# Moving the second half's x preparation into the u and g product, with GpSimd in program order during the first V product and staged scaling of B's weights

## The chip, the cores and the metric

The kernel runs on one core of one Trainium2 chip. The metric is the device time of one execution in microseconds, as the median of several runs. All times below are of that one core.

## The reference

A decoder trunk on x of 2048 tokens by 1024 features, in float32. One gated-MLP layer (A) is followed by one sliding-window attention layer (B). Cut to what matters here:

```python
h = rms_norm(x, a_norm_g)
u, v, g = split(h @ w_in, 3)            # w_in: 1024 x 6144, each part 2048 wide
v = layer_norm(v, ln_g, ln_b)           # over 2048 features
sv = einsum('gts,bcsgd->bctgd', tril(ws), v) + bs   # mixes the tokens of a chunk of 128, 16 groups
x = x + (u * sv * silu(g)) @ w_out
kv = rms_norm(x, kv_norm_g) @ w_kv + b_kv           # layer B from here
z  = rms_norm(x, b_norm_g) @ b_w_in                 # q and gate
... rotary, banded attention with sinks, gate, output product
out = rms_norm(x, final_norm_g)
```

The norm gains kv_norm_g and b_norm_g are multiplied into the weights w_kv and b_w_in ahead of layer B ("B's weights scaled").

## The kernel before

Every large product is made in three matmuls with operands split into a high part (rounded to the matmul's own type) and a low part (the rest): high times high, high times low, low times high. `split` makes them: a copy on ACT (L118) and a subtraction on DVE (L119). PE, DVE, ACT and POOL are TensorE, VectorE, ScalarE and GpSimd; SP is the queue that carries all loads, in order.

Layer A goes over the tokens in two halves of 1024. For each half come the V product, the u/g product (8 pairs of feature blocks; gate and mixing of the pair before are woven in) and the out product (4 pairs). The first V product (`vphase_first`, 768 matmuls of 128x512) works plainly on x split as it comes; the later products use Winograd's form of Strassen's 2x2 scheme: 7 products for 8, on sums and differences of quarters of x and of the weights. Those sums of quarters have to be prepared, and most of it is done beside the first V product:

- `sum_job(i)`, four of them: loads four quarters of wv into the tile pair qa, makes four sums or differences on GpSimd (`quarter_sums`) and stores them (su) for the V product of the second half.
- `x_steps(0, k)`: x of the first half, rebuilt from its high and low part on GpSimd (L448) and multiplied by the norm factor on DVE (L449), then 7 stores of plain quarters and their combinations (`combos`, GpSimd; X and X_s are the stores).
- `x_steps(1, k)`: the same for the second half, but loaded from memory into tile xq and normalised on DVE (L445), with the factor loaded from rx.
- `stat_steps(b)`: loads x of the second half, squares it on ACT, adds the squares on DVE (L248), and ends in `rnorm`, a chain over PE, DVE, GpSimd and ACT that gives the norm factor (L255 to L291).
- `load_consts(q)`: masks the mixing weights, forms a constant, stores 32 small pieces (wsc).

Beside the second V product (`vphase(1)`, 672 matmuls) 36 jobs `prescale(i)` scale B's weights: a multiplication on GpSimd (L496), the high part on ACT (L499), the low part on GpSimd (L502), two stores (L504).

Two things set the order. The program counts half steps: `half()` is called after each 12 matmuls and runs what `after(n, ...)` has put n half steps ahead. A scheduler then turns the program's order into one queue for each engine, by the readiness that it expects. Tiles named s come from a pool of 18 that rotates; raw weights have 12 buffers, split weights 4, and `weights()` keeps three splits ahead. The first V product is half steps 0 to 64, a u/g pair 14 half steps.

```python
        for i in range(4):
            after(6 + 6 * i, lambda i=i: sum_job(i))
```

Of the kernel before, what the change touches and what calls it, by code (L numbers as in the profile page):

```python
# [12 lines left out]
F32 = mybir.dt.float32  # L13
F32R = mybir.dt.float32r
I32 = mybir.dt.int32
AF = mybir.ActivationFunctionType
ALU = mybir.AluOpType

P = 128
# [3 lines left out]
TB = 512  # L23
# [3 lines left out]
NJ = AW // P  # L27
# [35 lines left out]
def trunk(ctx: ExitStack, tc: tile.TileContext, xT, wv, wug, wao, wkv, wqg, wbo, wsT, bs, gains, lngb,  # L63
# [12 lines left out]
    pD = [[dram.tile([P, TB], F32, name=f"p{b}_{k}", tag=f"p{b}_{k}") for k in range(KD)] for b in range(NB)]  # L76
    rxD = [dram.tile([P, TB], F32, name=f"rx{b}", tag=f"rx{b}") for b in range(NB)]
    vD = [[dram.tile([P, 2 * TT, 512], F32, name=f"v{i}_{c}", tag=f"v{i}_{c}") for c in range(4)] for i in range(2)]
    wscD = [dram.tile([P, 256], F32, name=f"wsc{j}", tag=f"wsc{j}") for j in range(NJ)]
    sumD = [[dram.tile([P, 2, 512], F32, name=f"su{i}_{n}", tag=f"su{i}_{n}") for n in range(4)] for i in range(4)]  # L80
    setD = {(s, i): {n: dram.tile([P, 4, TB], F32, name=f"{s}{i}_{n}", tag=f"{s}{i}_{n}") for n in STEPS}
            for s in ("X", "Y0_", "Y1_") for i in range(2)}
# [5 lines left out]
    def load(dst, src):  # L88
        nc.sync.dma_start(dst, src)

    def slot(dt=F32):
        return gen[0].tile([P, TB], dt, name="s", tag="s")
# [24 lines left out]
    def split(hi, lo, src, lo_eng=None):  # L117
        A.copy(hi, src)  # L118
        (lo_eng or V).tensor_tensor(lo, src, hi.bitcast(F32), ALU.subtract)  # L119
# [22 lines left out]
    def after(n, fn):  # L142
        at(now[0] + n, fn)
# [18 lines left out]
    for b in range(NB):  # L162
        for p in PIECES:
            kind, i, j = p[0], int(p[1]), int(p[2])
# [78 lines left out]
    def sumsq_step(acc, src, eng=G):  # L243
        sq = slot()
        A.activation(sq, src, AF.Square)
        if acc is None:
            return sq
        eng.tensor_tensor(acc, acc, sq, ALU.add)  # L248
        return acc
# [83 lines left out]
    with ExitStack() as actx:  # L333
# [51 lines left out]
        def load_consts(q):  # L385

            w, c = slot(), slot()
            w3 = w.rearrange("p (j t) -> p j t", j=4)
            load(w3, wsT[:, 4 * q:4 * q + 4, :])
            load(c, bs[q * 512:(q + 1) * 512].partition_broadcast(P))  # L390

            def first():
                G.affine_select(out=w3, in_=w3, pattern=[[0, 4], [1, P]], base=0, channel_multiplier=-1,
                                compare_op=ALU.is_ge, fill=0.0)

            def second():
                ps = bank()
                PE.matmul(ps, ones, w, start=True, stop=True)
                for i in range(4):
                    ts, j = slice(i * P, (i + 1) * P), 4 * q + i  # L400
                    V.scalar_tensor_tensor(c[:, ts], ps[:, ts], ln_b[:, j:j + 1], c[:, ts], ALU.mult, ALU.add)
                    G.dma_start(wscD[j][:, :P], w[:, ts])
                    G.dma_start(wscD[j][:, P:], c[:, ts])

            after(2, first)
            after(5, second)
# [17 lines left out]
        def x_steps(sb, k, tag):  # L424

            qs, its = [], []

            def begin():
                t = xcg.tile([P, 2048], F32, name="xq", tag=tag)
                qs.extend(t[:, i * TB:(i + 1) * TB] for i in range(4))  # L430
                if sb:
                    for i, z in enumerate(qs):
                        load(z, xT[2 + i // 2, k + 4 * (i % 2)])
                    rs.extend(slot() for _ in range(2))
                    for h in range(2):
                        load(rs[h], rxD[2 + h])
                else:
                    rs.extend(r0[h] for h in range(2))

            rs = []  # L440

            def norm(i):
                h, n = i // 2, k + 4 * (i % 2)
                if sb:
                    V.scalar_tensor_tensor(qs[i], qs[i], a_g[:, n:n + 1], rs[h], ALU.mult, ALU.mult)  # L445
                else:
                    hi, lo = fx[h, n]
                    G.tensor_tensor(qs[i], hi.bitcast(F32), lo.bitcast(F32), ALU.add)  # L448
                    V.tensor_tensor(qs[i], qs[i], rs[h], ALU.mult)  # L449

            def norms(h):
                norm(2 * h)
                norm(2 * h + 1)

            def step():
                if not its:
                    its.append(combos(qs[0], qs[2], qs[1], qs[3], ("X", sb), k))
                next(its[0])

            return [begin, lambda: None, lambda: norms(0), lambda: norms(1), step, step, step]  # L460

        def sum_job(i):

# [6 lines left out]
                sumD[i][n], t.rearrange("p (u c) -> p u c", u=2))))  # L470

        def quarter_sums(a11, a12, a21, a22, put):
            G.tensor_tensor(a22, a21, a22, ALU.add)
            put(0, a22)
            G.tensor_tensor(a21, a11, a21, ALU.subtract)
            put(2, a21)
            G.tensor_tensor(a11, a22, a11, ALU.subtract)
            put(1, a11)
            G.tensor_tensor(a12, a12, a11, ALU.subtract)
            put(3, a12)  # L480


# [4 lines left out]
        def prescale(i):  # L487
            src, dst, g, nk = pre_jobs[i // 2]
            nk //= 2
            z = i % 2  # L490
            w = slot()
            load(w, src[:, z * 512:(z + 1) * 512])

            def second():
                w3 = w.rearrange("p (k n) -> p k n", k=nk)
                G.tensor_tensor(w3, w3, g[:, z * nk:(z + 1) * nk, None].broadcast_to([P, nk, 512 // nk]), ALU.mult)  # L496
                for i, t in enumerate((slot(F32R), slot(F32R))):
                    if i == 0:
                        A.copy(t, w)  # L499
                        hi = t  # L500
                    else:
                        G.tensor_tensor(t, w, hi.bitcast(F32), ALU.subtract)  # L502
                for i, t in enumerate((hi, t)):
                    G.dma_start(dst[:, i * 1024 + z * 512:i * 1024 + (z + 1) * 512], t.bitcast(F32))  # L504

            after(2, second)


        def chain_of(width, product, keep, done, on_step):
# [101 lines left out]
        def load_v(sb, j):  # L611
            v = vtile().rearrange("p (c d) -> p c d", c=2 * TT)
            load(v, vD[sb][j // 4][:, :, (j % 4) * P:(j % 4 + 1) * P])
            wc = ac.tile([P, 256], F32, name="wc", bufs=3)
            load(wc, wscD[j])
            return v, wc

        def mix(j, ln, v, wc, us, sgs):
# [123 lines left out]
            fx[h, k] = hi, lo  # L742

        box = [None, None]

        def first_stat(h, k, t, wait):
            box[h] = sumsq_step(box[h], t, V)
            if k == KD - 1:
                rnorm(box[h], lambda r: r0.update({h: r}), wait, 4, lambda z: r4.update({h: z}))

# [12 lines left out]
            after(3 + k // 2, lambda k=k: first_split(1, k, ys[k]))  # L763
            after(6 + k // 2, lambda k=k: first_stat(1, k, ys[k], 2))
        for i in range(4):
            after(6 + 6 * i, lambda i=i: sum_job(i))
        for k in range(4):
            for i, f in enumerate(x_steps(0, k, ("12h", "12l")[k % 2])):
                after(18 + 6 * k + i, f)
            for i, f in enumerate(x_steps(1, k, ("s2h", "s2l")[k % 2])):  # L770
                after(38 + 6 * k + i, f)
        for b in range(2, 4):
            for i, f in enumerate(stat_steps(b)):
                after(10 + 8 * (b - 2) + i, f)
        for q in range(4):
            after(14 + 4 * q, lambda q=q: load_consts(q))
        for i, n in ((50, "11"), (53, "12"), (58, "s1"), (60, "s3"), (62, "s2")):
# [3 lines left out]
        for sb in range(2):  # L781
            if sb:
                for i in range(36):
                    after(3 + 3 * i // 2, lambda i=i: prescale(i))
                ln = vphase(sb)
            else:
                ln = vphase_first()
                load_set(("X", 0), "s4")
                load_set(("X", 0), "22")
            pend = None  # L790
            res = {}

            def ahead(kh, m, sb=sb, res=res):
                res[11] = res_loads(sb, kh, m, 11)

            for kh in range(2):
                for jj in range(4):
                    last = kh == 1 and jj == 3
                    pend = ug_pair(sb, kh, jj, ln, pend, ("Y0_", sb) if last else None, (lambda: ahead(0, 0)) if last else None)
            acc = [None, None]  # L800
            for kh in range(2):
                for m in range(2):
                    nxt = None
                    if m == 1:
                        nxt = ("Y1_", sb) if kh == 0 else ("X", 1) if sb == 0 else None
                    if sb and kh and m:
                        hn0 = ([], [])
                        for k, f in enumerate(hn_steps(0, *hn0)):
                            after(6 + k, f)
                    nx = 2 * kh + m + 1  # L810
                    out_pair(sb, kh, m, acc, nxt, pend, ln, res, (lambda: ahead(nx // 2, nx % 2)) if nx < 4 else None)
                    pend = None
            for h in range(2):
                rnorm(acc[h], lambda r, b=2 * sb + h: G.dma_start(rD[b], r))
# [419 lines left out]
```

## Time and profile before

| | us |
|---|---|
| median of 3 runs | 2284.58 |
| lowest and highest | 2279.96, 2290.11 |
| the profiled execution | 2290.78 |
| its span, from first to last instruction | 2288.9 |

| engine | busy us | share of the span |
|---|---|---|
| PE (matmul) | 2152.2 | 94% |
| DVE | 1678.9 | 73% |
| ACT | 1086.0 | 47% |
| POOL | 1137.0 | 50% |

The mean granted clock of TensorE is 0.976 of full speed, and 441.95 MB go through DMA at a mean of 193 GB/s. In the profile a group names the code line, the engine, the operation, the tiles (written to, then read from) and how often; behind the bar stand the busy time in us and the mean in ns, and last the idle time of the engine just before the group with what ended it. A row of waits names engine, tile and line that waited, what it waited for, and the total, the number and the longest. A row of transfers ends with its size in KB and the median time in us from issue to landing. Matmuls overlap, so their distance is read from their starts.

### The profile page before, as it was taken

The page shows a single profiled execution, that of the slowest core. Times are in us where ns is not written, and L with a number is a line of the kernel's source. Part 1 is how long each engine was busy: PE and PEld are TensorE (multiplying, and loading weights), DVE is VectorE, ACT ScalarE, POOL GpSimd, SP SyncE. Part 2 cuts the span into 40 slices and gives each one's busy share as a digit, 9 for nine tenths or more (in the row PEclk, how much of TensorE's full clock was granted, in tenths as well). Part 3 has the DMA queues.
Part 4 walks back from the last instruction along what each step waited for, and adds up shares of the span by engine and source line. Part 5 has one row for each costly group of instructions (what it writes and reads, how often), then busy time and mean ns, then how long its engine had stood idle before and what let it go on. Part 6 is the DMA issues. An engine that isn't in the chain of part 4 may idle for free.

```text
span 2288.9 us, 33545 instructions
## 1 busy us (share of the span) xinstructions
PE 2152.2 (94%) x11196; PEld 1816.8 (79%) x11196; DVE 1678.9 (73%) x2641; ACT 1086.0 (47%) x2431; POOL 1137.0 (50%) x1238
## 2 busy tenths in 40 slices
PE   6878899999999998999999999989999999999997
PEld 4656678888878776778888778889889889989986
DVE  8787866576888856666667788667957876895785
ACT  5322454454624533345445534436725744672673
POOL 5786535454455477955445454515513532551461
PEclk8988999999999999999999999999999999999999
DMA  7997834344777778934444677643355255336322
GB/s 275 339 334 267 310 108 157 110 153 143 239 272 252 275 244 292 315 113 152 128 136 154 213 263 250 233 158 111 116 193 181 88 195 188 111 120 219 132 93 92
DMA packets 209324, 441.95 MB, mean 193 GB/s; under 512 B 23040, under 2 KB 62208, under 8 KB 199936
## 3 DMA queue, kind: packets, MB, share of 16 engines
q1 hardware_dynamic: 163488, 255.76, 34.5%
q0 software_dynamic: 41056, 175.67, 21.1%
q10 hardware_dynamic: 4608, 8.39, 1.0%
q8 instruction: 89, 1.46, 0.3%
q14 instruction: 83, 0.68, 0.1%
HBM read 322.81 MB, written 116.92 MB: 192 GB/s over the span
## 4 chain that ended last, share of the span: by engine, by line
PE 62%; DVE 12%; DMA 11%; POOL 6%; issue 6%; ACT 3%; SPq 1%; DVEq 0%; POOLq 0%; ACTq 0%
PE ps L130 12%; PE ps L128 12%; PE ps L129 12%; PE ps L122 6%; PE ps L124 6%; PE ps L123 6%; PE ps L625 2%; DMA s<-in_xT 2%; DVE wa L119 2%; PE ps L997 2%; DMA s<-in_wqg 1%; DVE xl L119 1%; DMA s<-X_s 1%; PE ps L975 1%; POOL s L502 1%
## 5 line engine op out<-in xcount | busy, mean ns | idle before, releaser
L119 DVE TENSOR_TENSOR wa<-w_raw,wa 128x512 fp32r<-128x512 f32 x456 | 481.7, 1068 | 223.5 <-ACT wa L118 218.2
L130 PE MATMUL ps<-xh,wa 128*128 128x512 f32 x1344 | 530.3, 395 | 15.1 <-DVE wa L119 15.1
L128 PE MATMUL ps<-xh,wa 128*128 128x512 f32 x1344 | 531.7, 396 | 6.0 <-ACT s L539 4.2
L129 PE MATMUL ps<-xl,wa 128*128 128x512 f32 x1344 | 528.9, 394 | 0.0
L118 ACT CAST wa<-w_raw 128x512 fp32r<-128x512 f32 x456 | 279.4, 619 | 395.3 <-PE ps L130 296.5
L130 PEld LDWEIGHTS ps<-xh,wa 128*128 128x128 f32 x1344 | 253.7, 189 | 76.7 <-DVE wa L119 20.4
L128 PEld LDWEIGHTS ps<-xh,wa 128*128 128x128 f32 x1344 | 253.9, 189 | 62.0 <-ACT s L539 4.6
L129 PEld LDWEIGHTS ps<-xl,wa 128*128 128x128 f32 x1344 | 253.8, 189 | 55.8
L983 POOL TENSOR_SCALAR_AFFINE_SELECT s<-s 128x512 fp32r<-128x512 f32 x256 | 185.3, 752 | 101.6 <-ACT s L977 69.3
L122 PE MATMUL ps<-w,hn 128*128 128x256 f32 x640 | 184.3, 288 | 0.0
L123 PE MATMUL ps<-w,hn 128*128 128x256 f32 x640 | 182.4, 285 | 0.0
L124 PE MATMUL ps<-w,hn 128*128 128x256 f32 x640 | 182.3, 285 | 0.0
L223 POOL TENSOR_TENSOR w_raw<-w_raw 128x512 f32<-128x512 f32 x48 | 73.6, 1534 | 201.4 <-DMA w_raw<-in_wug 134.0
L123 PE MATMUL ps<-wa,xh 128*128 128x512 f32 x256 | 109.9, 429 | 43.4 <-DVE wa L119 43.4
L119 DVE TENSOR_TENSOR xl<-s,xh 128x512 fp32r<-128x512 f32 x168 | 138.8, 866 | 11.0 <-ACT xh L118 10.8
L190 POOL DMA_DIRECT2D w<-wb x72 | 40.7, 566 | 205.6 <-PE ps L124 181.5
L225 POOL TENSOR_TENSOR w_raw<-w_raw 128x512 f32<-128x512 f32 x48 | 71.0, 1482 | 124.0 <-DVE wa L119 123.9
L621 ACT ACTIVATE vp<-vp,nb,rs 128x128 f32<-128x128 f32 x256 | 106.3, 484 | 49.2 <-DMA vp<-v 35.1
L969 POOL TENSOR_TENSOR s<-s,rd 128x512 f32<-128x512 f32 x64 | 69.6, 1090 | 117.0 <-DVE rd L967 47.7
L123 PEld LDWEIGHTS ps<-w,hn 128*128 128x128 f32 x640 | 124.2, 194 | 0.5
L122 PEld LDWEIGHTS ps<-w,hn 128*128 128x128 f32 x640 | 124.0, 194 | 0.5
L124 PEld LDWEIGHTS ps<-w,hn 128*128 128x128 f32 x640 | 124.0, 194 | 0.0
(195 smaller groups left out, 5057.2 us busy)
## 6 DMA issues: line engine op xcount, KB each, us to landing
w<-wb POOLq DMA_DIRECT2D x72, 1024.0 KB, 5.4
w_raw<-in_wug SPq DMA_DIRECT2D x160, 256.0 KB, 3.1
w_raw<-in_wv SPq DMA_DIRECT2D x88, 256.0 KB, 5.8
w_raw<-in_wao SPq DMA_DIRECT2D x80, 256.0 KB, 4.2
wb<-s POOLq DMA_DIRECT2D x72, 256.0 KB, 4.8
s<-in_xT SPq DMA_DIRECT2D x64, 256.0 KB, 5.6
vp<-v SPq DMA_DIRECT2D x32, 512.0 KB, 4.4
Y_s<-s POOLq DMA_DIRECT2D x64, 256.0 KB, 3.8
```

Source lines behind the costliest of these rows:

```text
L118: A.copy(hi, src)
L119: (lo_eng or V).tensor_tensor(lo, src, hi.bitcast(F32), ALU.subtract)
L122: PE.matmul(ps, ah, bh, start=first, stop=False)
L123: PE.matmul(ps, ah, bl, start=False, stop=False)
L124: PE.matmul(ps, al, bh, start=False, stop=last)
L128: PE.matmul(ps, ah, bh, start=first, stop=False, skip_group_check=True)
L129: PE.matmul(ps, ah, bl, start=False, stop=False, skip_group_check=True)
L130: PE.matmul(ps, al, bh, start=False, stop=True, skip_group_check=True)
L223: G.tensor_tensor(u["22"], u["21"], u["22"], ALU.add)
L225: G.tensor_tensor(u["11"], u["22"], u["11"], ALU.subtract)
L621: A.activation(v[:, c, :], v[:, c, :], AF.Identity, bias=nb[:, c:c + 1], scale=rs[:, c:c + 1])
L983: G.affine_select(out=y.rearrange("p (h q) -> p h q", h=4), in_=x.rearrange("p (h q) -> p h q", h=4), pattern=[[0, 4], [sign, P]], base=ba ...
```

## The change

Four edits. (1) `x_steps(1, k)` and `stat_steps(2)`, `stat_steps(3)` are put into the first half's u/g product: the statistics into pairs 0 to 2, the preparation of x, one k for each pair, into pairs 3 to 6. Their tiles are now taken from the rotating pool s. (2) A new helper `in_turn` chains GpSimd's tensor operations in the order of the program: the sums of wv (now in two pieces of 512 columns for one of 1024), the rebuilding of x, and, for the second block of the first half, the square sums, which move from DVE to GpSimd (L770 in the changed kernel). `sum_job(i)` is put 14 + 9i half steps ahead for 6 + 6i, `x_steps(0, k)` 17 + 8k for 18 + 6k, and it has one empty step more between the tile and the normalisation. (3) `load_consts` stores 8 pieces of 256 KB for 32 of 64 KB. (4) `prescale` is taken apart: the multiplication two half steps after the load, the split a half step later, with the low part on DVE, the stores yet one later.

```diff
-    wscD = [dram.tile([P, 256], F32, name=f"wsc{j}", tag=f"wsc{j}") for j in range(NJ)]
+    wscD = [dram.tile([P, 4, 2, P], F32, name=f"wsc{q}", tag=f"wsc{q}") for q in range(4)]
...
-                    G.dma_start(wscD[j][:, :P], w[:, ts])
-                    G.dma_start(wscD[j][:, P:], c[:, ts])
+                for i, z in enumerate((w, c)):
+                    G.dma_start(wscD[q][:, :, i, :], z.rearrange("p (j t) -> p j t", j=4))
...
+                if sb == 0:
+                    t = xcg.tile([P, 2048], F32, name="xq", tag=tag)
+                    qs.extend(t[:, i * TB:(i + 1) * TB] for i in range(4))
+                else:
+                    qs.extend(slot() for _ in range(4))
...
-                    G.tensor_tensor(qs[i], hi.bitcast(F32), lo.bitcast(F32), ALU.add)
+                    in_turn(lambda: G.tensor_tensor(qs[i], hi.bitcast(F32), lo.bitcast(F32), ALU.add))
...
-            return [begin, lambda: None, lambda: norms(0), lambda: norms(1), step, step, step]
+            return [begin, lambda: None, lambda: None, lambda: norms(0), lambda: norms(1), step, step, step]
...
         def quarter_sums(a11, a12, a21, a22, put):
-            G.tensor_tensor(a22, a21, a22, ALU.add)
+            def tt(out, a, b, op):
+                for z in range(2):
+                    zs = slice(z * 512, (z + 1) * 512)
+                    in_turn(lambda: G.tensor_tensor(out[:, zs], a[:, zs], b[:, zs], op))
+
+            tt(a22, a21, a22, ALU.add)
...
-            def second():
-                w3 = w.rearrange("p (k n) -> p k n", k=nk)
-                G.tensor_tensor(w3, w3, g[:, z * nk:(z + 1) * nk, None].broadcast_to([P, nk, 512 // nk]), ALU.mult)
-                for i, t in enumerate((slot(F32R), slot(F32R))):
-                    if i == 0:
-                        A.copy(t, w)
-                        hi = t
-                    else:
-                        G.tensor_tensor(t, w, hi.bitcast(F32), ALU.subtract)
-                for i, t in enumerate((hi, t)):
-                    G.dma_start(dst[:, i * 1024 + z * 512:i * 1024 + (z + 1) * 512], t.bitcast(F32))
-            after(2, second)
+            w3 = w.rearrange("p (k n) -> p k n", k=nk)
+            gb = g[:, z * nk:(z + 1) * nk, None].broadcast_to([P, nk, 512 // nk])
+            after(2, lambda: G.tensor_tensor(w3, w3, gb, ALU.mult))
+            def third():
+                hi, lo = slot(F32R), slot(F32R)
+                split(hi, lo, w)
+                def fourth():
+                    for i, t in enumerate((hi, lo)):
+                        G.dma_start(dst[:, i * 1024 + z * 512:i * 1024 + (z + 1) * 512], t.bitcast(F32))
+                after(1, fourth)
+            after(3, third)
...
+        def in_turn(fn):
+
+            if gl[0] is None:
+                gl[0] = fn().ins
+                return
+            with tc.issue_after(gl[0]):
+                gl[0] = fn().ins
...
         def first_stat(h, k, t, wait):
-            box[h] = sumsq_step(box[h], t, V)
+            if h and box[1]:
+                sq = slot()
+                A.activation(sq, t, AF.Square)
+                in_turn(lambda: G.tensor_tensor(box[1], box[1], sq, ALU.add))
+            else:
+                box[h] = sumsq_step(box[h], t, V)
...
-            after(6 + 6 * i, lambda i=i: sum_job(i))
+            after(14 + 9 * i, lambda i=i: sum_job(i))
...
-                after(18 + 6 * k + i, f)
-            for i, f in enumerate(x_steps(1, k, ("s2h", "s2l")[k % 2])):
-                after(38 + 6 * k + i, f)
-        for b in range(2, 4):
-            for i, f in enumerate(stat_steps(b)):
-                after(10 + 8 * (b - 2) + i, f)
+                after(17 + 8 * k + i, f)
...
+            if sb == 0:
+                for b in range(2, 4):
+                    for i, f in enumerate(stat_steps(b)):
+                        after(3 + 16 * (b - 2) + 3 * i // 2, f)
+                for k in range(4):
+                    for i, f in enumerate(x_steps(1, k, None)):
+                        after(14 * (k + 3) + 5 + i, f)
```

How the queues of the engines change is shown at three places. The lines of the changed kernel have other numbers: the sums of wv L479 (before L473 to L479), their stores L472 (L469), the rebuilding of x L451 (L448), its multiplication L452 (L449), the statistics of v L607 (L597).

GpSimd (POOL) early in the first V product, before; qa and su are the sums and their stores, xq<-xh,xl the rebuilding of x, r the power in a norm chain:

```order
L448 TENSOR_TENSOR xq<-xh,xl 128x512 x6
L119 TENSOR_TENSOR s<-s 128x512
L448 TENSOR_TENSOR xq<-xh,xl 128x512 x2
L473 TENSOR_TENSOR qa<-qa 128x1024
L469 DMA su_0_165<-qa 128x1024
L260 TENSOR_TENSOR r_486<-m_483,neghalf 128x4
L475 TENSOR_TENSOR qa<-qa 128x1024
L469 DMA su_2_167<-qa 128x1024
L477 TENSOR_TENSOR qa<-qa 128x1024
L469 DMA su_1_166<-qa 128x1024
```

Now the same place:

```order
L770 TENSOR_TENSOR s<-s 128x512 x7
L479 TENSOR_TENSOR qa<-qa 128x512 x3
L119 TENSOR_TENSOR s<-s 128x512
L472 DMA su_0_153<-qa 128x1024
L479 TENSOR_TENSOR qa<-qa 128x512 x2
L472 DMA su_2_155<-qa 128x1024
L260 TENSOR_TENSOR r_650<-m_647,neghalf 128x4
L479 TENSOR_TENSOR qa<-qa 128x512 x2
L472 DMA su_1_154<-qa 128x1024
L479 TENSOR_TENSOR qa<-qa 128x512
L451 TENSOR_TENSOR xq<-xh,xl 128x512
```

The rebuilding of x came first and all at once; it now stands behind the sums of the first job, and each later piece behind those of a later job.

DVE in the middle of the first V product, before, with the square sums (L248), a norm chain (L255 to L282) and the constants (L401) between the weight splits (L119):

```order
L248 TENSOR_TENSOR s<-s 128x512
L255 TENSOR_TENSOR s<-ps,ident 128x512
L257 TENSOR_REDUCE m_1074<-s 128x4
L258 TENSOR_SCALAR m_1074<-m_1074 128x4
L119 TENSOR_TENSOR wa<-w_raw,wa 128x512
L277 CAST r4h<-r_1077 128x4
L279 TENSOR_TENSOR r4l<-r_1077,r4h 128x4
L282 TENSOR_TENSOR s<-ident,r4h 128x512
L282 TENSOR_TENSOR s<-ident,r4l 128x512
L119 TENSOR_TENSOR wa<-w_raw,wa 128x512
```

Now, at the third piece of x:

```order
L401 SCALAR_TENSOR_TENSOR s<-ps,lngb_sb,s 128x128 x4
L119 TENSOR_TENSOR wa<-w_raw,wa 128x512 x2
L452 TENSOR_TENSOR xq<-xq,s 128x512
L119 TENSOR_TENSOR wa<-w_raw,wa 128x512
L452 TENSOR_TENSOR xq<-xq,s 128x512 x3
L119 TENSOR_TENSOR wa<-w_raw,wa 128x512
```

The second half's square sums and norm chains are gone from this stage; the multiplications of x (L452), which wait for GpSimd's L451, stand between the weight splits.

GpSimd in the second V product, before, with what each row waits for:

```order
L496 TENSOR_TENSOR s<-s,g_sb 128x512 [waits DMAHW7_49]
L502 TENSOR_TENSOR s<-s 128x512 [waits Activation_49]
L504 DMA wb_225<-s 128x512 [waits DMASW2_49]
L504 DMA wb_225<-s 128x512 [waits DMASW3_49,Pool_49]
L502 TENSOR_TENSOR s<-s 128x512 [waits DMASW4_49,Activation_49]
```

Now (L504 is the multiplication, L512 the stores):

```order
L504 TENSOR_TENSOR s<-s,g_sb 128x512 [waits DMAHW6_49]
L512 DMA wb_212<-s 128x512 [waits DMASW4_49,Activation_49]
L512 DMA wb_212<-s 128x512 [waits DMASW5_49,DVE_49]
L504 TENSOR_TENSOR s<-s,g_sb 128x512 [waits DMAHW7_49]
L512 DMA wb_212<-s 128x512 [waits DMASW6_49,Activation_49]
L512 DMA wb_212<-s 128x512 [waits DMASW7_49,DVE_49]
```

The subtraction has left GpSimd's queue, and the store of the low part waits for DVE instead.

More of the change, by code (lines that the diff above doesn't have):

```diff
@@ L428, in begin @@
             def begin():
-                t = xcg.tile([P, 2048], F32, name="xq", tag=tag)
-                qs.extend(t[:, i * TB:(i + 1) * TB] for i in range(4))
+                if sb == 0:
[3 more added lines that the diff above has]
+                    qs.extend(slot() for _ in range(4))
                 if sb:
@@ L472, in quarter_sums @@
         def quarter_sums(a11, a12, a21, a22, put):
-            G.tensor_tensor(a22, a21, a22, ALU.add)
+            def tt(out, a, b, op):
[3 more added lines that the diff above has]
+            tt(a22, a21, a22, ALU.add)
             put(0, a22)
-            G.tensor_tensor(a21, a11, a21, ALU.subtract)
+            tt(a21, a11, a21, ALU.subtract)
             put(2, a21)
-            G.tensor_tensor(a11, a22, a11, ALU.subtract)
+            tt(a11, a22, a11, ALU.subtract)
             put(1, a11)
-            G.tensor_tensor(a12, a12, a11, ALU.subtract)
+            tt(a12, a12, a11, ALU.subtract)
             put(3, a12)
@@ L614, in load_v @@
             wc = ac.tile([P, 256], F32, name="wc", bufs=3)
-            load(wc, wscD[j])
+            load(wc.rearrange("p (i t) -> p i t", i=2), wscD[j // 4][:, j % 4])
             return v, wc
@@ L744, in trunk @@
         box = [None, None]
-        def first_stat(h, k, t, wait):
-            box[h] = sumsq_step(box[h], t, V)
+        gl = [None]
+        def in_turn(fn):
[4 more added lines that the diff above has]
+                gl[0] = fn().ins
+        def first_stat(h, k, t, wait):
+            if h and box[1]:
[4 more added lines that the diff above has]
+                box[h] = sumsq_step(box[h], t, V)
             if k == KD - 1:
```

## The prediction

> **What bounds the kernel now.** I read three views in this order: the busy time in stretches, then the groups and waits of the two V products, then the transfers. The columns of the first: stretch, length, busy time of PE, PEld, DVE, ACT and POOL, granted clock, DMA share, GB/s. The stretches are the V product of the first half, its u/g product, its out product, the V product of the second half, and all the rest.
>
> ```profile
> 0.00:288.00 288.00, 220.56 (x840) 170.04 (x840) 240.68 (x256) 105.26 (x180) 191.64 (x197) 0.89 0.87 305
> 288.00:605.00 317.00, 312.88 (x1470) 260.15 (x1471) 209.89 (x249) 157.98 (x318) 145.23 (x133) 0.99 0.44 138
> 605.00:784.00 179.00, 172.29 (x756) 139.82 (x755) 146.97 (x196) 84.92 (x151) 88.69 (x85) 0.99 0.76 265
> 784.00:973.00 189.00, 167.29 (x681) 131.18 (x680) 118.54 (x142) 74.92 (x139) 150.10 (x181) 0.95 0.84 289
> 973.00:2289.00 1316.00, 1279.22 (x7452) 1115.64 (x7451) 962.85 (x1802) 662.96 (x1646) 561.30 (x644) 0.99 0.47 158
> ```
>
> PE is full in u/g, the out product and the rest. It is not in the two V products. The first holds 768 large matmuls. How fast these can follow each other, and what a wait costs beyond itself, the timeline shows:
>
> ```profile
> 49.46 0.79 PE L123 MATMUL ps<-wa,xh 128*128 128x512 f32 x1 [11.95 <-DVE wa L119]
> 50.48 0.63 PE L123 MATMUL ps<-wa,xh 128*128 128x512 f32 x1
> 50.91 0.63 PE L124 MATMUL ps<-wa,xl 128*128 128x512 f32 x1
> 54.44 0.39 PE L124 MATMUL ps<-wa,xl 128*128 128x512 f32 x1
> 54.67 0.39 PE L122 MATMUL ps<-wa,xh 128*128 128x512 f32 x1
> ```
>
> After a gap of 11.95 us they start 0.43 us apart (50.48 to 50.91), and some 4 us later 0.23 us apart (54.44 to 54.67). So V1, as I call the first V product, would take 768 x 0.23 = 177 us from its start at about 6 us, against 282. V2, the second, would take 672 x 0.23 = 155 us, against 189. The waits and groups of V1 say what stands between:
>
> ```profile
> PE ps L123 <- DVE wa L119: 43.4, 11, 11.9
> SPq L89 <- DMA su<-qa: 51.4, 7, 20.1
> L119 DVE TENSOR_TENSOR wa<-w_raw,wa 128x512 fp32r<-128x512 f32 x68 | 92.7, 1390 | 4.5 <-ACT wa L118 4.5
> L248 DVE TENSOR_TENSOR s<-s 128x512 f32<-128x512 f32 x28 | 29.1, 1040 | 10.6 <-ACT s L245 9.9
> L445 DVE SCALAR_TENSOR_TENSOR xq<-xq,g_sb,s 128x512 f32<-128x512 f32 x16 | 15.0, 967 | 14.6 <-DMA s<-rx 9.5 <-DMA s<-X 5.1
> L282 DVE TENSOR_TENSOR s<-ident,r4l 128x512 fp32r<-128x512 f32 x4 | 13.1, 3268 | 0.0
> L277 DVE CAST r4h<-r 128x4 fp32r<-128x4 f32 x4 | 8.6, 2153 | 3.9 <-POOL r L260 3.9
> ```
>
> PE waits for the low part of a split weight (43.4 us). The splits run on DVE, which is busy 240.7 of 288 us (84%) and itself sits idle behind transfers when it gets to the normalisation of the second half's x.
>
> **The change, part by part: V1.** Three things leave it or alter in it.
>
> DVE: the 16 normalising operations (15.0 us), 21 of the 28 square sums (14 go to u/g and 7 to GpSimd: 21 x 1.04 = 21.8) and two of the four norm chains (of each I count the two longest rows, 3.27 + 2.15 = 5.4, so 10.8) go. 240.7 - 47.6 = 193 us. At the share of 84% that DVE reaches now, V1 would last 193 / 0.84 = 230 us.
>
> Transfers: of V1's bytes these go.
>
> ```profile
> DMA packets 43818, 87.98 MB, mean 305 GB/s; under 512 B 5500, under 2 KB 7932, under 8 KB 43802
> s<-in_xT SPq DMA_DIRECT2D x32, 256.0 KB, 5.8
> xq<-in_xT SPq DMA_DIRECT2D x16, 256.0 KB, 7.3
> X_s<-s POOLq DMA_DIRECT2D x24, 256.0 KB, 4.0
> X<-s POOLq DMA_DIRECT2D x8, 256.0 KB, 5.0
> s<-rx SPq DMA_DIRECT2D x8, 256.0 KB, 5.8
> 50.00:100.00 50.00, 44.23 (x173) 34.49 (x171) 43.10 (x52) 18.56 (x33) 33.24 (x30) 0.93 0.96 343
> ```
>
> Half of the 32 loads of x (4.2 MB), the 16 loads for the normalisation (4.2), the 8 loads of its factor (2.1) with their two stores (0.5), and 28 of the 56 stores of X (first and last of four rows above; 7.3): 18.3 MB of 88.0. The remaining 69.7 MB at 305 GB/s take 229 us, at the 343 GB/s of the fullest stretch 203 us.
>
> GpSimd: its tensor operations now run in the order of the program. Behind the chain stand the additions that rebuild x (L451), and DVE's multiplication by the norm (L452) waits for them in DVE's queue, with the next weight splits, which PE waits for, behind it. The rows for a walk along the chain:
>
> ```profile
> L379 POOL TENSOR_TENSOR s<-xq 128x512 f32<-128x512 f32 x8 | 10.3, 1286 | 0.0
> L448 POOL TENSOR_TENSOR xq<-xh,xl 128x512 f32<-128x512 f32 x16 | 25.0, 1578 | 13.4 <-DVE xl L741 13.4
> L469 POOL DMA_DIRECT2D su<-qa x16 | 9.1, 572 | 2.1 <-POOL qa L473 0.9 <-POOL qa L477 0.6 <-POOL qa L475 0.3
> su<-qa POOLq DMA_DIRECT2D x16, 512.0 KB, 6.9
> qa<-in_wv SPq DMA_DIRECT2D x16, 512.0 KB, 6.1
> L402 POOL DMA_DIRECT2D wsc<-s x16 | 8.9, 556 | 0.3 <-POOL s L393 0.3
> ```
>
> A job of quarter sums is 8 additions of half the old width (1.29 us, as L379) and 4 stores (0.57); the next job has the same buffers, so it loads when the stores have landed (6.9) and adds when its loads have (6.1): 10.3 + 2.3 + 13.0 = 25.6 us each. The first job's sums are due in half step 16, at about 16 x 3.6 = 57 us (3.6: a pace of 230 us over 64 steps). The third job then ends at 57 + 3 x 25.6 = 134 us. The additions for the third piece of x are behind it in GpSimd's order, due in step 36, where PE at full speed could be at 6 + 36 x 2.8 = 107 us: up to 27 us of waiting for DVE's queue. From 134 the fourth job ends at 134 + 4 x 1.58 + 25.6 = 166 us, and the fourth piece's additions are at 172, where step 44 would be at 134 + 8 x 2.8 = 156. Twenty steps remain: 172 + 20 x 2.8 = 228, and with a slow clock after each of the stalls (about 4 us at half speed, so 2 us each) and the first waits I put the end of V1 at 234, near the ends of the two sums above. That is **-54 us**. Bounds: 205 us (-83), where transfers at 343 GB/s are all that is left, and 268 (-20), where the stalls of the chain come on top of some of the present ones.
>
> Constants in 8 stores for 32: 24 x 0.56 = 13 us fewer on GpSimd, which has 288 - 192 = 96 us idle in V1. I cost this at nothing; without that cover it is at most 13 us of the chain just walked, in its favour.
>
> **u/g.** What left V1 comes here: DVE 15.0 + 14 x 1.04 + 10.8 = 40 us onto 209.9 of 317, and 18.3 MB onto 138 GB/s (44%), which gives about 196 GB/s. PE barely waits here now, GpSimd does, for weights:
>
> ```profile
> L128 PE MATMUL ps<-xh,wa 128*128 128x512 f32 x416 | 164.9, 396 | 4.2 <-ACT s L539 4.2
> POOL w_raw L223 <- DMA w_raw<-in_wug: 66.1, 13, 6.5
> ```
>
> The cover of the moved work is DVE's 107 idle us. It isn't complete: in V1, PE waited 43.4 us for DVE on 240.7 us of DVE work, 0.18 us for each. By that 40 us of work cost 7 us: **+7 us**. Bounds: 0 (the cover is whole, as it is for today's 210 us) and +20 (half of the added DVE time on PE's path, when several such operations stand together ahead of a split).
>
> **V2.** Today multiply (L496), high copy (ACT, L499), low subtraction (L502) and the two stores of a piece of B's weight stand together:
>
> ```profile
> ACT s L499 <- POOL s L496: 93.8, 26, 8.9
> PE ps L128 <- ACT wa L118: 10.2, 4, 5.2
> PE ps L129 <- DVE wa L119: 6.5, 7, 2.5
> L502 POOL TENSOR_TENSOR s<-s 128x512 fp32r<-128x512 f32 x34 | 45.4, 1336 | 3.6 <-ACT s L499 3.4
> L496 POOL TENSOR_TENSOR s<-s,g_sb 128x512 f32<-128x512 f32 x36 | 39.1, 1096 | 18.1 <-DMA s<-in_wqg 17.7
> L119 DVE TENSOR_TENSOR wa<-w_raw,wa x56: 669/693/4144, 786.4 to 972.2; 128x512 fp32r<-128x512 f32 x56
> L119 DVE TENSOR_TENSOR wa<-w_raw,wa 128x512 fp32r<-128x512 f32 x56 | 69.0, 1266 | 66.4 <-ACT wa L118 63.9 <-DMA w_raw<-in_wug 2.3
> ```
>
> ACT stands 93.8 us behind GpSimd's multiplications, with the weight copies queued behind it. With a half step between, those multiplications are done when ACT comes to the copies, so most of PE's 10.2 us behind ACT should go, and with them about half of the lost clock (0.95 against 0.99 over 189 us is 7 us; 3.5 of it). DVE keeps its own waits: 36 subtractions at 0.69 to 1.27 us come to it, 25 to 46 us on 118.5, at most 164 of 189. GpSimd loses 45.4. I take 10.2 + 3.5, less 2 for what DVE adds: **-12 us**. Bounds: -24 (all 16.7 us of both waits and the clock's 7) and +8 (46 us of DVE work at 0.18).
>
> The row of tile wa has a minimum of 0.67, a median of 0.69 and a mean of 1.27 us: some splits take twice to six times as long as others of the same shape. The Trainium skill, SBUF — State Buffer, section "Who interferes with whom", says that a DVE operation with two inputs in SBUF and a GpSimd operation that reads SBUF shut each other out for a whole instruction. The mean above the median agrees. By that rule taking L502 off GpSimd frees DVE too: the excess of 56 x (1.27 - 0.69) = 32 us lies beside 45.4 + 39.1 us of GpSimd operations (L502 and L496), so 17 us of it go; with the new subtractions at 0.69, DVE would be busy 118.5 + 25 - 17 = 126 us, and V2 would be nearer the -24 than the -12.
>
> **Sum.** -54 + 7 - 12 = -59 us. The profiled execution took 2290.8 us (span 2288.9), 6 us over the median of the runs, so it would become 2231.8; against the median of 2284.6 I say 2226. Changes under 0.5% (11 us) can't be told from none here.
>
> **Rivals.** (a) *Both V products get close to PE's own pace*: V1 at its -83, u/g 0, V2 at -24: -107, so 2178. For it: DVE at 193 us and the transfers at 203 allow it. Against: the chain of quarter sums and DVE's multiplications.
>
> (b) *GpSimd's order keeps V1 long.* What the walk has as stalls at two places comes at all four jobs, because a job also waits on SP's queue (51.4 us behind the stores of sums today). V1 at -25, u/g +7, V2 nothing: -18, so 2266.
>
> (c) *No change.* The round trips of the four jobs still set V1: they begin 8 half steps later (14 for 6) and follow at 9 instead of 6 steps, so SP's 51.4 us remain, and the bytes saved are only idle time of the transfers. V1 -7, u/g +7: within 11 us of 2285. Against: the fullest stretch at a share of 0.96 says that bytes matter.
>
> (d) *Slower, by SP's queue in u/g.* The x of the second half is now in 18 rotating slots, and SP issues all loads in order. Where a load of x waits for a slot that a store of X still holds, the weight loads queued behind it wait too. The cover is 12 raw and 3 split weights of 12 matmuls each, 15 x 12 x 0.23 = 41 us at most; u/g's 4.2 us of waiting says that it's deep today. To undo the rest it must cost 59 + 11 = 70 us, that is four pieces of x, each blocked some 41 + 18 us. The median store lands in 4 to 5 us, which speaks against it. It would give about 2300.
>
> **Chances.** Forecast (2203 to 2250) 0.55; (a) 0.14, (b) 0.16, (c) 0.08, (d) 0.07. The range of 2168 to 2268 holds the forecast, (a) and about two thirds of (b): 0.80. Faster is the forecast, (a) and (b), 0.85; same (c), 0.08; slower (d), 0.07.
>
> **What would show it.** V1 ends at about 234 us with some 70 MB and DVE busy some 193 us there; its stalls are DVE's L452 waiting for GpSimd's L451 about 107 to 134 us and before 172. u/g takes 317 to 330 us with no PE wait over some 10 us in sum there. V2 takes about 177 us, with ACT's wait for GpSimd's multiplication (now L504) far under 93.8 us. From the out product of the second half on nothing changes. The prediction is wrong if V1 stays over 260 us, if u/g grows by more than 20, or if V2 doesn't shrink because DVE has become what PE waits for.

## The result and the profile after

The changed kernel takes 2229.8 us (median of 4 runs, 2226.8 to 2234.5) against 2284.9 us, a ratio of 0.9758 with a 95% interval of 0.974 to 0.9775. The prediction was 2226. The profiled execution of the changed kernel took 2234.5 us, the one of the kernel before 2290.8; both lie at the upper end of their runs, so their difference (56 us) can be split by stage.

The busy time in stretches, columns as in the prediction; the stretches are again V1, u/g, out product, V2 and the rest, cut at the places where PE now goes from one to the next:

```profile
0.00:235.00 235.00, 202.23 (x795) 156.73 (x796) 168.26 (x201) 94.62 (x158) 144.85 (x144) 0.93 0.85 291
235.00:555.00 320.00, 319.43 (x1506) 265.15 (x1505) 259.47 (x293) 167.16 (x338) 192.27 (x185) 1.00 0.60 194
555.00:740.00 185.00, 177.79 (x775) 143.92 (x774) 153.14 (x203) 87.66 (x154) 85.20 (x86) 0.98 0.76 265
740.00:926.00 186.00, 169.18 (x694) 135.44 (x693) 139.45 (x184) 81.13 (x144) 117.08 (x155) 0.94 0.84 298
926.00:2233.00 1307.00, 1272.50 (x7434) 1112.36 (x7432) 949.30 (x1793) 658.06 (x1638) 553.12 (x633) 0.99 0.47 158
```

DVE fell from 240.7 of 288 us to 168.3 of 235 in V1 and rose from 209.9 to 259.5 in u/g, where PE stayed full. In V1 PE stood idle 67.4 us before and 32.8 us now. Cuts by eye differ by some us between kernels, so for the sums below I compare the start of the same large matmul (L122 to L130) in each trace. They are counted from the first of the program, and they alone, because the change moves eight small matmuls of norm chains out of V1. V1 has 768 large matmuls; its stretch here goes on to the 877th, that is 108 matmuls into the first u/g pair, so that the hand-over counts. u/g goes to the 2,053rd, the out product to the 2,821st, V2 to the 3,777th, and the rest to the start of the last matmul.

| us by the same matmuls | V1 | u/g | out | V2 | rest |
|---|---|---|---|---|---|
| before | 301.8 | 295.2 | 189.3 | 262.0 | 1226.8 |
| changed | 251.7 | 298.1 | 191.2 | 252.2 | 1226.1 |
| difference | -50.1 | +2.9 | +1.9 | -9.8 | -0.7 |

One trace gives a stage only to some us: the kernels below that do not touch V1 differ from their base there by 2 to 3 us, and V2 of the ten kernels that share the new scaling lies between 245.5 and 254.7 us.

The waits and groups of V1 in the changed kernel; the third row is that of the weight splits:

```profile
DVE xq L452 <- POOL xq L451: 28.7, 3, 14.4
PE ps L123 <- DVE wa L119: 20.9, 8, 7.8
L119 DVE TENSOR_TENSOR wa<-w_raw,wa 128x512 fp32r<-128x512 f32 x69 | 84.0, 1237 | 20.7 <-ACT wa L118 20.7
L479 POOL TENSOR_TENSOR qa<-qa 128x512 f32<-128x512 f32 x32 | 43.6, 1388 | 1.8 <-DMA qa<-in_wv 1.7
DMA packets 34816, 68.77 MB, mean 291 GB/s; under 512 B 3949, under 2 KB 6381, under 8 KB 34802
```

PE's wait for the low part of a weight halved (43.4 to 20.9 us). The new wait that the prediction walked along is there: DVE stands 28.7 us behind GpSimd's additions of x. The timeline puts its two long pieces at the third and fourth piece of x (start, length, and in brackets the idle time before it):

```profile
128.81 1.31 POOL L451 TENSOR_TENSOR xq<-xh,xl 128x512 f32<-128x512 f32 x1
130.15 0.96 DVE L452 TENSOR_TENSOR xq<-xq,s 128x512 f32<-128x512 f32 x1 [12.31 <-POOL xq L451]
159.25 1.25 POOL L451 TENSOR_TENSOR xq<-xh,xl 128x512 f32<-128x512 f32 x1
160.54 1.17 DVE L452 TENSOR_TENSOR xq<-xq,s 128x512 f32<-128x512 f32 x1 [14.41 <-POOL xq L451]
```

In V2, ACT's wait for the multiplication on GpSimd fell from 93.8 to 40.4 us, PE no longer waits for ACT there, and its wait for the low part of a weight grew from 6.5 to 13.4:

```profile
ACT s L118 <- POOL s L504: 40.4, 19, 6.3
PE ps L129 <- DVE wa L119: 13.4, 5, 7.6
```

### The profile page after: what moved, and what is told of

Read it like the earlier page. It is cut to its first block, busy times and chain, and to the rows that moved or that the text cites. A ratio compares the mean times of both kernels' runs of the same rounds, so it can differ in the third digit from the quotient of the medians.

```text
span 2232.8 us, 33563 instructions
## 1 busy us (share of the span) xinstructions
PE 2141.1 (96%) x11196; PEld 1813.6 (81%) x11196; DVE 1669.6 (75%) x2670; ACT 1088.6 (49%) x2431; POOL 1092.5 (49%) x1201
## 4 chain that ended last, share of the span: by engine, by line
PE 72%; DVE 10%; DMA 7%; issue 5%; POOL 4%; ACT 2%; SPq 1%; POOLq 0%; DVEq 0%; ACTq 0%
PE ps L130 13%; PE ps L129 13%; PE ps L128 13%; PE ps L122 8%; PE ps L123 8%; PE ps L124 8%; PE ps L635 2%; PE ps L1024 2%; DVE wa L119 1%; PE ps L971 1%; PE ps L1002 1%; PE ps L972 1%; PE ps L943 1%; DMA s<-Y 1%; POOL qa L479 1%
## 5 line engine op out<-in xcount | busy, mean ns | idle before, releaser
L119 DVE TENSOR_TENSOR wa<-w_raw,wa 128x512 fp32r<-128x512 f32 x456 | 478.7, 1059 | 148.0 <-ACT wa L118 147.0
L130 PE MATMUL ps<-xh,wa 128*128 128x512 f32 x1344 | 529.4, 394 | 14.7 <-DVE wa L119 14.7
L130 PEld LDWEIGHTS ps<-xh,wa 128*128 128x128 f32 x1344 | 253.3, 188 | 74.8 <-DVE wa L119 18.4
L122 PE MATMUL ps<-w,hn 128*128 128x256 f32 x640 | 184.5, 288 | 0.0
L119 DVE TENSOR_TENSOR xl<-s,xh 128x512 fp32r<-128x512 f32 x168 | 137.7, 856 | 13.7 <-ACT xh L118 13.6
L123 PE MATMUL ps<-wa,xh 128*128 128x512 f32 x256 | 107.1, 418 | 21.2 <-DVE wa L119 20.9
L122 PEld LDWEIGHTS ps<-w,hn 128*128 128x128 f32 x640 | 124.2, 194 | 0.5
```

What stands on the lines that cost most here:

```text
L122: PE.matmul(ps, ah, bh, start=first, stop=False)
L123: PE.matmul(ps, ah, bl, start=False, stop=False)
L130: PE.matmul(ps, al, bh, start=False, stop=True, skip_group_check=True)
```

## The experiments

Times are medians; ratios, with their 95% interval, are to the kernel before, timed on the same chip as the experiment. The experiments ran on several chips, so two of them are best compared by their ratios. Stage times are by the same matmuls as above, each from one trace.

**The parts alone.** The theory was that V1 is shorter because DVE's work and bytes leave it; the rival, that GpSimd's order does it.

Part 1, on the kernel before:

```diff
-            for i, f in enumerate(x_steps(1, k, ("s2h", "s2l")[k % 2])):
-                after(38 + 6 * k + i, f)
-        for b in range(2, 4):
-            for i, f in enumerate(stat_steps(b)):
-                after(10 + 8 * (b - 2) + i, f)
...
+            if sb == 0:
+                for b in range(2, 4):
+                    for i, f in enumerate(stat_steps(b)):
+                        after(3 + 16 * (b - 2) + 3 * i // 2, f)
+                for k in range(4):
+                    for i, f in enumerate(x_steps(1, k, None)):
+                        after(14 * (k + 3) + 5 + i, f)
```

(with the tiles of the second half's x from the pool s)

> The kernel before with one part of the change alone: the statistics and x of the second half prepared in the u and g product. Theory (the first V product is shorter because work of DVE and bytes leave it): it ends 35 to 45 us earlier, the u and g product is at most 3 us longer, about 2242 us in all. Rival (what counts is GpSimd's order): at most 15 us of gain, 2270 us or more.

Measured: 2258.4 us, 0.9878 (0.9859 to 0.9897). V1 -38.0, u/g +4.3, out +2.8, V2 +2.5. V1 did what the theory said; u/g lost a little more than its 3 us, and the total gained less than forecast.

Part 2, on the kernel before:

```diff
-                    G.tensor_tensor(qs[i], hi.bitcast(F32), lo.bitcast(F32), ALU.add)
+                    in_turn(lambda: G.tensor_tensor(qs[i], hi.bitcast(F32), lo.bitcast(F32), ALU.add))
...
-            after(6 + 6 * i, lambda i=i: sum_job(i))
+            after(14 + 9 * i, lambda i=i: sum_job(i))
...
-                after(18 + 6 * k + i, f)
+                after(17 + 8 * k + i, f)
```

(with `in_turn`, the new `quarter_sums` and the new `first_stat` of the change)

> The kernel before with GpSimd's program order alone (with the narrower sums, the later jobs and the square sums of the second block on GpSimd). Theory (work and bytes): the first V product keeps its length or gets longer, since DVE's multiplications of x wait some 29 us for GpSimd and nothing left but 7 additions: 2280 to 2295 us. Rival (order): 2250 to 2265 us.

Measured: 2281.7 us, 0.9979 (0.9969 to 0.9989). V1 -10.7. In time it lies where the theory put it, but V1 did get shorter, which the theory did not allow; a small gain of its own.

Part 4, on the kernel before:

```diff
...
-            after(2, second)
+            after(2, lambda: G.tensor_tensor(w3, w3, gb, ALU.mult))
+            def third():
+                hi, lo = slot(F32R), slot(F32R)
+                split(hi, lo, w)
...
+                after(1, fourth)
+            after(3, third)
```

> The kernel before with the staged scaling of B's weights alone. Theory (ACT no longer stands behind GpSimd's multiplication, and the low parts are cheap on DVE): the second V product with its hand-over is 8 to 12 us shorter, 2274 us. Rival (the 10 us came from something else, DVE takes as much as ACT gives): 2282 to 2287 us.

Measured: 2276.1 us, 0.9952 (0.9934 to 0.9969). V2 -15.3 in the profiled execution. The gain in V2 is that of this part: the ten kernels with the staged scaling and the low part on DVE have a V2 of 245.5 to 254.7 us, the three with the old scaling 262.0 to 264.5. The -15.3 here and the -9.8 of the changed kernel lie within that spread.

Part 3, taken back from the changed kernel:

```diff
-                for i, z in enumerate((w, c)):
-                    G.dma_start(wscD[q][:, :, i, :], z.rearrange("p (j t) -> p j t", j=4))
+                    G.dma_start(wscD[j][:, :P], w[:, ts])
+                    G.dma_start(wscD[j][:, P:], c[:, ts])
```

(with the tiles in memory and their loads as before)

> The changed kernel with the constants in 32 stores as before. Theory (GpSimd, busy over 44 of 50 us between 50 and 150 us, is the one DVE waits for there, so 13 us of issuing come back on its queue): first V product 3 to 8 us longer, 2233 to 2238 us. Rival (hidden): within 2 us, 2228 to 2232 us.

Measured: 2239.7 us, 0.9794 (0.9773 to 0.9815); V1 258.5 for 251.7. PE's wait for DVE is 29.4 us for 20.9. The stores aren't hidden, though the two intervals touch: 0.9775 and 0.9773. Why they cost this is not shown: DVE's wait for GpSimd's additions of x, which the theory expected to grow, is 24.7 us for 28.7. The four parts by their ratios: 28 + 5 + 11 (each alone) + 8 (taken back) = 52 of the 55 us.

**The chain alone**, taken out of the changed kernel:

```diff
-            with tc.issue_after(gl[0]):
-                gl[0] = fn().ins
+            gl[0] = fn().ins
```

> The changed kernel without the chain on GpSimd (all else as changed). Theory A (the chain is what makes DVE's multiplications of x wait 28.7 us and the splits behind them): the first V product is 10 to 20 us shorter, 2212 to 2222 us. Rival B (without it the scheduler puts the rebuilding of x ahead of everything, and the first norm chain and the sums come late): 2233 to 2250 us.

Measured: 2240.2 us, 0.9801 (0.9784 to 0.9817), V1 255.7. It is slower, as rival B has it. The wait for GpSimd's additions fell only to 20.9, and PE's first norm product now waits 10 us that it didn't:

```profile
DVE xq L452 <- POOL xq L451: 20.9, 2, 12.1
PE ps L270 <- ACT s L118: 10.8, 2, 10.0
```

**Bytes or DVE's work?** Two doses into V1 of the changed kernel.

```diff
+        dump = [dram.tile([P, TB], F32, name=f"dump{i}", tag=f"dump{i}") for i in range(56)]
+        for i in range(56):
+            after(5 + i, lambda i=i: nc.sync.dma_start(dump[i], xT[2 + i // 28, i % 8]))
```

> The changed kernel with 56 copies of 256 KB from memory to memory added in the first V product, one each half step, 14.7 MB that no instruction waits for; they are work that the reference doesn't need. Theory (bytes bound the stage): 14.7 MB at some 305 to 343 GB/s are 43 to 48 us, half or more of them seen: 2252 to 2275 us. Rival (DVE and GpSimd bound it, the transfers have room): 2228 to 2240 us.

Measured: 2236.6 us (2225.6 to 2238.8), 0.9768 (0.9742 to 0.9793); V1 249.5. The dose's transfers of the first 230 us:

```profile
DMA packets 36011, 82.37 MB, mean 358 GB/s; under 512 B 4779, under 2 KB 7211, under 8 KB 35101
```

The transfers took the dose on top (358 GB/s for 291) and V1 isn't longer. Bytes don't bound it, so the part of the first theory that rests on bytes falls. The dose goes from memory to memory; what loads into tiles cost beyond that it doesn't test.

```diff
+        spare = ac.tile([P, 480], F32, name="spare")
+        V.memset(spare, 0.0)
+        for i in range(56):
+            after(5 + i, lambda: V.tensor_tensor(spare, spare, spare, ALU.mult))
```

> The changed kernel with 56 additional products of 128x480 on DVE in the first V product, one each half step, of a tile that nothing else uses; some 0.65 us each alone, 36 us or more in all. Theory (DVE's work bounds the stage): 20 to 36 us longer, 2250 to 2266 us. Rival (bytes or GpSimd's chain bound it and DVE has room in its waits): under 8 us, 2228 to 2238 us.

Measured: 2266.3 us, 0.9912 (0.9897 to 0.9928); V1 284.0, that is +32.3. Time in DVE's queue does lengthen V1. The group of the dose:

```profile
L798 DVE TENSOR_TENSOR spare<-spare 128x480 f32<-128x480 f32 x56 | 82.9, 1480 | 1.1
```

I had expected 0.65 us each. The mean is 1.48 because there are two kinds: the 31 that overlap with no tensor operation of GpSimd took 0.65 us, the other 25 took 2.50 in the mean. So 82.9 us came into DVE's queue, not 36, and V1 got 32.3 us longer: the rest came out of DVE's wait for GpSimd's additions (28.7 to 1.1 us) and out of the weight splits (84.0 to 59.5), against a new wait of 13.2 us behind a store of sums.

The statistics back into V1, in the changed kernel:

```diff
+        for b in range(2, 4):
+            for i, f in enumerate(stat_steps(b)):
+                after(10 + 8 * (b - 2) + i, f)
```

(and out of u/g)

> The changed kernel with the statistics of the second half (16 loads, 14 square sums and two norm chains on DVE) back in the first V product; x itself stays in the u and g product. Theory (DVE's work counts as much as bytes): 4.2 MB and some 25 us of DVE come back, the first V product is 12 to 20 us longer, 2242 to 2250 us. Rival (bytes are what counts): 4.2 of 18.3 MB, 8 to 12 us longer, 2238 to 2242 us. Rival (GpSimd's chain sets the length): under 5 us.

Measured: 2248.2 us, 0.9822 (0.9805 to 0.9838); V1 270.6, +18.9. That is as the theory on DVE has it; the rivals on bytes and on the chain fall. Since bytes alone did nothing, about half of part 1's gain is the work of the statistics, most of it on DVE; ACT's squares came back with it. The other half came with x itself, and no run separates DVE's normalisation of x from GpSimd's combinations of it.

**Is DVE's wait for GpSimd what remains?** Two ways to shorten it in the changed kernel.

```diff
-                    V.tensor_tensor(qs[i], qs[i], rs[h], ALU.mult)
+                    after(3, lambda: V.tensor_tensor(qs[i], qs[i], rs[h], ALU.mult))
```

(with the stores three half steps later)

> The changed kernel with DVE's multiplications of the first half's x (and the stores behind them) three half steps after GpSimd's additions. Theory (DVE bounds the first V product, so its 28.7 us of waiting for GpSimd in that queue are paid in full or nearly): the wait falls under 12 us and the stage is 10 to 18 us shorter, 2212 to 2220 us. Rival (the wait is time that DVE has, because the splits behind it are ahead of PE): within 4 us of the changed kernel, 2226 to 2234 us.

Measured: 2228.8 us, 0.9747 (0.9725 to 0.977), V1 250.3. This is the rival's number, but not by its reason:

```profile
DVE xq L452 <- POOL xq L451: 12.9, 3, 8.5
L119 DVE TENSOR_TENSOR wa<-w_raw,wa 128x512 fp32r<-128x512 f32 x68 | 100.0, 1493 | 21.4 <-ACT wa L118 21.4
```

The wait shrank by 15.8 us and the weight splits, 68 for 69, got 16 us longer (84.0 to 100.0). The same exchange shows in the dose of bytes, where the wait fell to 14.3 us and the splits took 102.0 in the first 230 us.

```diff
-                if sb:
-                    for i, z in enumerate(qs):
-                        load(z, xT[2 + i // 2, k + 4 * (i % 2)])
+                for i, z in enumerate(qs):
+                    load(z, xT[2 * sb + i // 2, k + 4 * (i % 2)])
...
-                    in_turn(lambda: G.tensor_tensor(qs[i], hi.bitcast(F32), lo.bitcast(F32), ALU.add))
-                    V.tensor_tensor(qs[i], qs[i], rs[h], ALU.mult)
+                V.scalar_tensor_tensor(qs[i], qs[i], a_g[:, n:n + 1], rs[h], ALU.mult, ALU.mult)
```

> The changed kernel with the first half's x loaded once more (16 loads, 4.2 MB) and normalised by one operation on DVE, in place of the addition on GpSimd and the multiplication on DVE. Theory (bytes have room, as 14.7 MB added cost the stage nothing; GpSimd is 23 us less busy and DVE no longer waits for it): first V product 12 to 20 us shorter, 2208 to 2220 us. Rival (the loads come late on the load queue, and DVE waits for them instead): within 5 us, 2225 to 2235 us.

Measured: 2226.9 us, 0.9744 (0.9719 to 0.977), V1 251.8. The rival holds: the wait only changed its name.

```profile
DVE xq L447 <- DMA xq<-in_xT: 30.6, 6, 17.3
POOL qa L474 <- DMA qa<-in_wv: 26.2, 4, 9.0
```

Neither is told apart from the changed kernel.

**GpSimd's additions themselves.** Leaving out the four sum jobs:

```diff
-        for i in range(4):
-            after(14 + 9 * i, lambda i=i: sum_job(i))
...
-            order += [wv[g, PLAIN.index(n), k] if n in PLAIN else sumD[2 * g + k // 2][int(n[1]) - 1][:, k % 2, :]
+            order += [wv[g, PLAIN.index(n) if n in PLAIN else 0, k]
```

> The changed kernel without the four jobs of quarter sums: the second V product takes plain quarters of wv in their place, so its values are not the reference's; its work is as before. It takes 44 us of GpSimd additions, 9 us of its issuing and 16.8 MB out of the first V product, and nothing from DVE. Theory (GpSimd's additions lengthen DVE's two-input operations and hold up its multiplications of x): the mean of a weight split falls from 1.24 to under 0.95 us and the first V product is 20 to 40 us shorter, 2190 to 2212 us. Rival (DVE's own work and PE's slow clock bound the stage): the splits' mean stays over 1.1 us and the stage within 8 us of the changed kernel's, 2222 to 2232 us.

Measured: 2203.5 us, 0.9618 (0.9594 to 0.9641), V1 222.2, -29.5. The splits and the waits of V1:

```profile
L119 DVE TENSOR_TENSOR wa<-w_raw,wa 128x512 fp32r<-128x512 f32 x70 | 67.6, 980 | 33.7 <-ACT wa L118 31.5 <-DMA w_raw<-in_wv 2.1
DVE xq L452 <- POOL xq L451: 11.8, 2, 7.9
L123 PE MATMUL ps<-wa,xh 128*128 128x512 f32 x256 | 102.9, 402 | 3.4 <-DVE wa L119 3.3
```

No work was taken from DVE, but a split's mean fell from 1.24 to 0.98 us (just above the 0.95 that I had set) and PE's wait from 20.9 to 3.3 us. It also took 16.8 MB away, which by the dose of bytes is not the reason, and its loads from the load queue, which no run separates.

The traces show the mechanism split by split. Of the 67 weight splits of V1 in the changed kernel, 37 overlap in time with no tensor operation of GpSimd, and each of these took 0.67 to 0.69 us. The other 30 took 1.96 us in the mean, the longest 6.61. Before, 33 without overlap took 0.67 to 0.69 us and 32 with it 2.15; without the sums 42 took 0.67 to 0.70 and 25 took 1.51. A split in a gap of GpSimd, and three splits beside its sums (start, length):

```profile
66.32 0.68 DVE L119 TENSOR_TENSOR wa<-w_raw,wa 128x512 fp32r<-128x512 f32 x1
85.39 8.91 DVE L119 TENSOR_TENSOR wa<-w_raw,wa 128x512 fp32r<-128x512 f32 x3
86.43 1.36 POOL L381 TENSOR_TENSOR s<-xq,s 128x512 f32<-128x512 f32 x1
88.84 2.58 POOL L479 TENSOR_TENSOR qa<-qa 128x512 f32<-128x512 f32 x2
91.92 1.83 POOL L479 TENSOR_TENSOR qa<-qa 128x512 f32<-128x512 f32 x1
```

The second of these three splits is the longest, from 85.99 to 92.60 us: it lasted through a row of several GpSimd operations. This also says why a wait that is scheduled away comes back: the splits that now run in its place run beside GpSimd.

**Where the low part of B's weights is made.** The changed kernel, staged, but on GpSimd:

```diff
-                split(hi, lo, w)
+                split(hi, lo, w, G)
```

> The changed kernel, staged scaling kept, but the low parts of B's weights subtracted on GpSimd again. Theory (the stages alone free ACT; the place of the subtraction matters little): second V product within 3 us of the changed kernel's, 2228 to 2233 us. Rival (GpSimd's subtractions lengthen DVE's two-input operations, so taking them off GpSimd was what helped): 6 to 12 us longer, 2236 to 2242 us, with the mean of a weight split back near 1.27 us in that stage.

Measured: 2237.9 us, 0.9783 (0.9768 to 0.9797); its interval overlaps with the changed kernel's, and its profiled V2 is 253.4 for 252.2. The time doesn't settle it. The splits do show the rival's mechanism: their mean in V2 is 1.44 us for 1.04, and 43 of the 57 overlap with GpSimd's tensor operations for 24. Minimum, median and maximum in ns in V2, first of the changed kernel, then of this one:

```profile
L119 DVE TENSOR_TENSOR wa<-w_raw,wa x57: 622/686/4331, 741.2 to 925.6; 128x512 fp32r<-128x512 f32 x57
```

```profile
L119 DVE TENSOR_TENSOR wa<-w_raw,wa x57: 675/1331/5946, 740.4 to 923.4; 128x512 fp32r<-128x512 f32 x57
```

## Why the prediction was right, point by point

- *V1, -54.* The end is where I put it: PE starts u/g at 232.6 us (234 said). But before, it started u/g at 276.8: the 288 us that I started from had 11 us of u/g in it. By the same matmuls, with the hand-over, the gain is 50.1 us. Alone, part 1 gives 38 and part 2 11, and the stores are worth 7; these are single traces, and their sum of 56 is over the 50.1. That DVE has less to do and V1 is shorter for it held; that the number came out so well is in good part luck, since the next three points, on which 234 rests, were each off in their reasons.
- *DVE's sum, 193 us.* Mis-sized: 168. The largest miss is the norm chains. I counted two rows of each, 10.8 us for two chains, but all their rows together fell from 37.3 to 12.1 us, since I left out the shorter rows and since the two chains that stayed got shorter too. The splits that stayed also got shorter (92.7 to 84.0). And DVE's share is 72%, not the 84% that I divided by. The two errors nearly cancel. That DVE's time is what the stage hangs on, the dose on DVE shows.
- *The bound by bytes, 229 us.* This step failed. The amount was right (69.7 MB said, 68.8 measured), but not that it bounds: 343 GB/s, my fullest stretch, was no ceiling, since with the dose the transfers went on at 358 over the whole stage, and V1 didn't move. That this sum met DVE's at about 230 us was chance.
- *The walk along GpSimd.* Its times were close: the third piece of x was due at 134 and came at 128.8, the fourth at about 166 to 172 and came at 159.3. DVE waited 12.3 and 14.4 there (up to 27 and 16 said). The reason was another: I had the jobs wait 13 us for stores and loads to land, while GpSimd waited 1.7 us for loads of sums in all. It was busy with its own queue (44 of each 50 us between 50 and 150 us).
- *Constants, nothing.* Mis-sized, but within the bound given (13 us): about 8 us. The cover that I gave it, GpSimd's idle time, didn't hold; by which wait it is paid stays open.
- *u/g, +7.* It is +2.9, and +1.9 in the out product; 50 more us on DVE were nearly all covered. The share of V1 (0.18) doesn't hold in a stage where PE is full.
- *V2, -12.* It is -9.8, and -15.3 with part 4 alone. ACT's wait fell, PE's 10.2 us behind ACT went, and PE's wait for DVE took 7 us of it back.
- *The rivals.* (a) needed V1 to lose 83 us; without the sums it would be -79.6. (b) would have needed the stalls at all four jobs. (c) and (d) didn't come; PE doesn't wait for loads in u/g.

What the rule of the Trainium skill (SBUF — State Buffer, "Who interferes with whom") says, that DVE with two inputs in SBUF and GpSimd reading SBUF shut each other out, agrees with five traces: the changed kernel, where every split that overlaps with no tensor operation of GpSimd took at most 0.69 us; splits of 0.98 us without the sums for 1.24, of 1.49 where DVE no longer stood still while GpSimd added, a dose of which 25 of 56 took 2.50 us for 0.65, and a median of 1.33 in V2 with the low parts on GpSimd for 0.69. The sum of V1 leaned on bytes, which by the dose bound nothing here, and left this out.

## What to carry to other kernels

Ask of a full-looking stage which dose lengthens it: transfers at a share of 0.96 in their fullest stretch were no bound, and a dose on a DVE that is busy 72% lengthened the stage. Price GpSimd work not by its own time but by what it does to the two-input operations of DVE beside it; a wait for GpSimd that is scheduled away can come back as slower operations. Compare stages by the same instruction in both traces, and count only instructions that the change doesn't move; cuts by eye can have a piece of the next stage in them.

## What the runs showed of the hardware

- One core's transfers kept 358 GB/s over 230 us (291 without the dose), and V1 was no longer for it (249.5 us for 251.7).
- A split of 128x512 on DVE took 0.67 to 0.69 us wherever no tensor operation of GpSimd ran beside it (37 of 67 in V1 of the changed kernel). Beside them it took 1.96 us in the mean, and up to 6.61 when several GpSimd operations followed each other. A product of 128x480 of one tile took 0.65 us without, 2.50 with them.
